# Bank copies of ScalarE placed ahead of roundings, and residuals one product earlier, in a decoder block's second FFN projection

## The chip, the core and the metric

The kernel runs on one core of a Trainium2 chip. The metric is the device time of one execution in microseconds; before, it is 822.0 us, the median of three runs (821.88 to 822.13). The core's engines work side by side, each through its own queue of instructions in program order: TensorE (PE, matmuls; PEld is its weight load), VectorE (DVE), ScalarE (ACT), GpSimd (POOL) and SyncE (SP, which here only issues DMAs).

## What is computed

One decoder layer on 512 positions of width 1024: two mixers side by side, then a SwiGLU feed-forward network, then a final RMSNorm. The change touches the last part only, from the end of the first FFN matmul on:

```python
    h2 = rms_norm(x, norm2_g) * (1.0 + scale2) + shift2
    f_g, f_u = jnp.split(h2 @ w_ffn_in, 2, axis=-1)
    x = x + gate2 * ((jax.nn.silu(f_g) * f_u) @ w_ffn_out)
    return x
...
    return rms_norm(x, final_norm_g)
```

`w_ffn_out` has 2816 rows and 1024 columns. All of it is float32.

## The kernel before

**Precision.** A float32 product is made of three matmuls in a rounded format (`mm3`, lines 51 to 55). Each operand is split: `hi` is the value rounded, a copy by ScalarE; `lo` is the value less `hi`, a subtraction by VectorE. The matmuls are hi x hi, hi x lo and lo x hi, all adding into one PSUM bank. So every piece of weights and of activations needs a rounding on ScalarE and a subtraction on VectorE ahead of its matmuls.

**Weights.** `ensure` (119) walks a list of weight chunks of 512 KB. `issue` (72) starts the DMA of a chunk on SP into one of three buffers `raw`; `prep` (95) rounds it (line 112, ScalarE) and subtracts (line 116), into `hi` and `lo` of three buffers each. So a chunk's rounding can begin when the chunk three places before it has been multiplied, and a load when the subtraction of the chunk three places before it is done. `get(i, ahead)` (144) makes sure that chunk `i` and the `ahead` chunks behind it are prepared.

**First FFN projection.** The loop `for q in range(-2, NQ)` (1642), makes each group of columns by a Strassen-like scheme of seven products in place of eight (`sprod`, 1636). Partial sums are carried from one PSUM bank to the next: ScalarE copies bank `R[0]` into `R[1]` (1676) and `R[1]` into `R[2]` (1689), and TensorE adds the next product to the copy. The preparations for the next group, `pre`, are set between these steps; in the last group (q = 17) `pre` comes from `z_first` (1595), which prepares the second projection: the first three weight chunks (`b(0)` to `b(2)`) and the parts 0 to 2 of the activations `A11`, rounded by `a_hi` (1569; line 1585 in the profile) and subtracted by `a_lo` (1587; 1589). `a_sum` (1593 in the profile) makes a difference of two activation blocks for a later product.

**Second FFN projection.** Again seven products (`zprod`, 1760), in this order: A11, S1, S2, A12, S3, A22, S4. Each goes over six chunks of weights (c = 0 to 5; the last is half as long), and for each chunk over two halves e of 128 rows with 512 columns each. One chunk is 12 matmuls, the last 6. Ahead of the matmuls of chunk c stand `get`, which by default prepares the chunk two further on, and then a list of tasks written out by hand for that c: roundings, subtractions, sums, residuals. The results gather in the banks `Z[k][e]`. `z_copy` (1770) seeds a bank from another one; `z_out` (1775, the copy is line 1779) copies two banks, e = 0 and e = 1, to SBUF, because `z_add` (1781) needs them and TensorE goes on adding to the same banks. After product S3, `z_out(2)` does this, and product A22 adds to the same two banks `Z[2]`.

**Residual, norm and output.** For row block tk (128 rows) and column half h, `res_(tk, h)` (1827) runs `resid_v` (1234): VectorE multiplies the bank by the gate (1238) and adds into `xt[tk]` (1239); the square with its sum, on ScalarE (1240), is put on a list that `sq_` (1834) empties. `scale_g` (1724; 1730 in the profile) multiplies by the final norm's gain. `row_rstd` (1246) reduces the sums of a row block on VectorE (1247) and raises them to -1/2 on GpSimd (1248). `scaled(tk, n)` (1732) scales the row block: the columns from n on by ScalarE (1735), the first n by VectorE (1736); then it issues two output DMAs, one on SP and one on ScalarE's queue (1739). After the third chunk of S4 the last three chunks are prepared together (`ch`, 1844) and multiplied for row block 0 as a whole (512 columns) and for row block 1 in two halves of 256; for the second half a bank is copied first (1842). Each of these three is followed by its residual, and at the very end by `finish` (1741).

In a profile a helper's instructions carry the helper's line. The functions that the diff touches, with their line numbers:

Of the kernel before, what the change touches and what calls it, by code (L numbers as in the profile page):

```python
# [28 lines left out]
def block_kernel(ctx: ExitStack, tc: tile.TileContext, x, positions, w_ada, b_ada, w_in,  # L29
# [28 lines left out]
    stream, wseq, chunk = [], [], {}  # L58
# [60 lines left out]
    def ensure(upto):  # L119
        upto = min(upto, len(stream) - 1, st["limit"] - 1)  # L120
        while True:
            for i in range(st["prep"], min(st["prep"] + 16, len(stream), st["limit"])):
                if "raw" in stream[i]:
                    continue
                if room(i):
                    issue(i)
                elif stream[i]["kind"] == "w" or not stream[i]["mid"]:
                    break
            if st["prep"] > upto:
                break  # L130
# [139 lines left out]
    NZ = 6  # L270
# [3 lines left out]
    W_Z = {}  # L274
# [75 lines left out]
    def t512(name, dt=F32):  # L350
        return base.tile([128, 512], dt, name=name, tag="t512", bufs=3)
# [65 lines left out]
    gate_b = {1: base.tile([128, D], F32, name="gate1b", tag="gate", bufs=1)}  # L417
# [120 lines left out]
    for kt in range(8):  # L538
# [7 lines left out]
        kw = dict(skip_group_check=True)  # L546
# [687 lines left out]
    def resid_v(p, c0, n, slot, tk, gate):  # L1234

        cs_ = slice(c0, c0 + n)
        t = t512("rt")
        V.tensor_mul(t[:, :n], p, gate[:, cs_])
        V.tensor_add(xt[tk][:, cs_], xt[tk][:, cs_], t[:, :n])
        return lambda: A.activation(t[:, :n], xt[tk][:, cs_], AF.Square, scale=1.0 / 32,  # L1240
                                    accum_out=ss2[:, tk, slot:slot + 1])
# [4 lines left out]
    def row_rstd(tk):  # L1246
        V.tensor_reduce(r2[:, tk:tk + 1], ss2[:, tk], op=OP.add, axis=AX.X)
        P.tensor_tensor(r2[:, tk:tk + 1], r2[:, tk:tk + 1], mhalf[:, :1], op=OP.pow)
# [312 lines left out]
    def a_part(name, c):  # L1561
        kh, th = AT_[name]
        t = gz[((0, 1, 3, 5), (2, 4, 3, 5))[kh][c]]
        if c >= 2:
            n = 4 - c
            t = t[:, n * kh:n * kh + n]
        return t[:, :, th * 256:(th + 1) * 256]

    def a_hi(key, c):
        h = (ZA[key] + (None,))[c]  # L1570
        if c == 3:
            if not zl:
# [12 lines left out]
        A.activation(t[0], a_part(key, c), AF.Copy)  # L1585

    def a_lo(key, c):
        hi, lo = za[key, c]
        V.tensor_sub(lo, a_part(key, c), f(hi))

    def a_sum(key, c):
        x_, y_ = {"S1": ("A21", "A22"), "S2": ("A11", "S1"), "S3": ("S2", "A22"), "S4": ("A12", "S2")}[key]
        V.tensor_sub(*(a_part(n, c) for n in (key, x_, y_)))

    def z_first():
        def b(k):
            return lambda: ensure(wseq[wseq.index(W_Z[0, 0][0]) + k])
        st["limit"] = 1 << 30
        return [(b(0), lambda: a_hi("A11", 0), lambda: a_lo("A11", 0)),
                (b(1), lambda: a_hi("A11", 1), lambda: a_lo("A11", 1)),  # L1600
                (lambda: a_hi("A11", 2), lambda: (a_lo("A11", 2), a_sum("S2", 0))),
                (b(2), lambda: None)]


    pf = [[bank(b, "pf") for b in bs] for bs in ((0, 1), (2, 3))]
# [36 lines left out]
    for q in range(-2, NQ):  # L1642
        g, u = 2 + q // 2, q % 2
# [4 lines left out]
        S2_, S1_, A12, A22, S4_, S3_ = (half_of(d[k], e) for k in "CBD" for e in range(2))  # L1648
# [75 lines left out]
    def scale_g(c0, n, tk):  # L1724
        if not xo:
            for k in range(2):
                t = ffn[0].tile([128, 2, D], F32, name="xo", tag=f"E{k + 1}", bufs=1)
                xo.extend((t[:, 0], t[:, 1]))
        cs_ = slice(c0, c0 + n)
        V.tensor_mul(xo[tk][:, cs_], xt[tk][:, cs_], fng[0][:, cs_])  # L1730

    def scaled(tk, n):

        if n < D:
            A.activation(xo[tk][:, n:], xo[tk][:, n:], AF.Copy, scale=r2[:, tk:tk + 1])
        V.scalar_tensor_tensor(xo[tk][:, :n], xt[tk][:, :n], r2[:, tk:tk + 1], fng[0][:, :n],
                               op0=OP.mult, op1=OP.mult)
        for c, q in ((slice(0, 512), SY), (slice(512, D), A)):
            q.dma_start(out[tk * 128:(tk + 1) * 128, c], xo[tk][:, c])
# [8 lines left out]
    Z, ZB = {}, ((4, 7), (0, 1), (2, 3), (5, 6))  # L1748
# [8 lines left out]

    ALL = slice(0, 512)

    def zprod(k, ka, kw, start, tasks):  # L1760
        if start:
            Z[k] = [bank(ZB[k][e], "pfo") for e in range(2)]
        for c, i in enumerate(W_Z[kw][:len(tasks)]):
            w = get(i)
            for fn in tasks[c]:
                fn()
            for e in range(2):
                zmm(Z[k][e], ka, c, e, w, ALL, start and c == 0, c == NZ - 1)
# [3 lines left out]
        for e in range(2):  # L1772
            A.activation(Z[dst][e], Z[src][e], AF.Copy, scale=scale)

    def z_out(src):
        Z["s", src] = [t512("ps") if src == 3 else base.tile([128, 512], F32, name="ps", tag="acc", bufs=2)
                       for _ in range(2)]
        for e in range(2):
            A.activation(Z["s", src][e], Z[src][e], AF.Copy)  # L1779

    def z_add(dst, src, op):
        for e in range(2):
            op(Z[dst][e], Z[dst][e], Z["s", src][e])

    def hi_(key, c):
        return lambda: a_hi(key, c)

    def lo_(key, c):
        return lambda: a_lo(key, c)
# [10 lines left out]
    def load_fng():  # L1800
        fng.append(ffn[0].tile([128, D], F32, name="fng", tag="E0", bufs=1))
        P.dma_start(fng[0], rows_bcast(final_norm_g, D))

    zprod(0, "A11", (0, 0), True, [[outs_left, hi_("S1", 0)], [lo_("S1", 0), hi_("S1", 1), hi_("A11", 3)],
                                   [lo_("S1", 1), lo_("A11", 3), hi_("S1", 2), sm_("S2", 1)],
                                   [lo_("S1", 2), sm_("S1", 3), sm_("S2", 2), hi_("S2", 0)],
# [9 lines left out]
    zprod(0, "A12", (1, 0), False, [[lo_("A12", 3), hi_("S3", 2)], [lo_("S3", 2), lambda: z_add(1, 3, V.tensor_add)],  # L1816
                                    [hi_("A22", 0)], [lo_("A22", 0), hi_("A22", 1)], [lo_("A22", 1), hi_("A22", 2)],
                                    [lo_("A22", 2)]])
    zprod(2, "S3", 3, False, [[hi_("S3", 3), load_fng], [lo_("S3", 3), hi_("S4", 0)], [lo_("S4", 0), hi_("S4", 1)],
                              [lo_("S4", 1), hi_("S4", 2)], [lo_("S4", 2), hi_("A22", 3)], [lo_("A22", 3)]])  # L1820
    z_out(2)
    z_add(3, 2, V.tensor_sub)


    sq = []

    def res_(tk, h, g=True):
        def fn():
            sq.append(resid_v((Z[h] if tk < 2 else Z[2 + h])[tk % 2], 512 * h, 512, h, tk, gate_b[2]))
            if g:  # L1830
                scale_g(512 * h, 512, tk)
        return fn

    def sq_():
        while sq:
            sq.pop(0)()

    zprod(2, "A22", 4, False, [[res_(0, 0)], [sq_, res_(1, 0)], [sq_], [res_(2, 1)], [sq_, hi_("S4", 3)], [lo_("S4", 3)]])

    zprod(1, "S4", (1, 1), False, [[res_(3, 1, False)], [sq_, res_(2, 0, False)], [sq_, res_(3, 0, False)]])  # L1840
    last = bank(7, "pfo")
    A.activation(last[:, :256], Z[1][1][:, 256:], AF.Copy)
    ids = W_Z[1, 1][3:]
    ch = [get(i, 2 - k) for k, i in enumerate(ids)]
    sq_()
    row_rstd(2)
    row_rstd(3)
    scaled(2, 512)
    scaled(3, D)
    for tk in range(2):  # L1850
        for z in range(2) if tk else (None,):
            c = ALL if z is None else slice(256 * z, 256 * z + 256)
# [74 lines left out]
```

## Time and profile before

| | |
|---|---|
| median of three runs | 822.0 us (821.88 to 822.13) |
| the profiled execution | 823.29 us |
| its span, first to last instruction | 821.5 us |
| granted TensorE clock, mean | 0.998 |
| TensorE busy in the span | 805.9 us, 98% |
| VectorE / ScalarE / GpSimd busy | 686.6 / 430.9 / 166.6 us |

The trace is one execution. A row of a timeline reads: start in us from the span's start, duration in us, engine, line, operation, output tile and input tile with their shapes, count, and in brackets the idle time ahead of it and what ended that. Consecutive rows of one engine overlap by some hundredths or, on TensorE, by more, since instructions are pipelined; so times are also read from start to start. A row of the waits reads: engine, line, what it waited for, then the sum in us, how often, and the longest.

### The profile page before, as it was taken

The page shows a single profiled execution, that of the slowest core. Times are in us where ns is not written, and L with a number is a line of the kernel's source. Part 1 is how long each engine was busy: PE and PEld are TensorE (multiplying, and loading weights), DVE is VectorE, ACT ScalarE, POOL GpSimd, SP SyncE. Part 2 cuts the span into 40 slices and gives each one's busy share as a digit, 9 for nine tenths or more (in the row PEclk, how much of TensorE's full clock was granted, in tenths as well). Part 3 has the DMA queues.
Part 4 walks back from the last instruction along what each step waited for, and adds up shares of the span by engine and source line. Part 5 has one row for each costly group of instructions (what it writes and reads, how often), then busy time and mean ns, then how long its engine had stood idle before and what let it go on. Part 6 is the DMA issues. An engine that isn't in the chain of part 4 may idle for free.

```text
span 821.5 us, 12945 instructions
## 1 busy us (share of the span) xinstructions
PE 805.9 (98%) x4903; PEld 719.6 (88%) x4903; DVE 686.6 (84%) x1175; ACT 430.9 (52%) x772; POOL 166.6 (20%) x186
## 2 busy tenths in 40 slices
PE   7999999999999999999999999999999999999996
PEld 6789889988888888988888899999999999888875
DVE  7989798898899648888697879889999888898686
ACT  6674445322332226665635587555555655666554
POOL 3060031363344411000010010323121322000001
PEclk9999999999999999999999999999999999999999
DMA  9974352332346563037692603989997977556763
GB/s 294 301 222 111 111 180 78 104 102 79 106 150 198 166 200 102 28 104 247 195 254 48 205 27 103 227 236 250 255 280 196 247 182 207 172 190 201 219 175 134
DMA packets 108463, 141.35 MB, mean 172 GB/s; under 512 B 6689, under 2 KB 77089, under 8 KB 108209
## 3 DMA queue, kind: packets, MB, share of 16 engines
q1 hardware_dynamic: 97296, 110.41, 43.4%
q0 software_dynamic: 10384, 29.17, 15.0%
q10 hardware_dynamic: 720, 0.95, 0.3%
q8 instruction: 38, 0.62, 0.3%
q14 instruction: 25, 0.20, 0.1%
HBM read 138.15 MB, written 25.17 MB: 199 GB/s over the span
## 4 chain that ended last, share of the span: by engine, by line
PE 79%; DMA 7%; DVE 7%; ACT 4%; issue 1%; SPq 1%; POOL 0%; POOLq 0%; ACTq 0%; DVEq 0%
PE R L53 8%; PE R L54 8%; PE R L55 8%; PE pb L53 6%; PE pb L54 6%; PE pb L55 6%; PE pfo L53 4%; PE pfo L55 4%; PE pfo L54 4%; DMA mraw<-in_w_ada_dram 3%; PE pav L54 2%; PE pav L53 2%; PE pav L55 2%; DMA s<-in_w_ada_dram 2%; DMA oraw<-in_w_out_dram 2%; PE pgb L53 2%
## 5 line engine op out<-in xcount | busy, mean ns | idle before, releaser
L112 ACT ACTIVATE hi<-raw 128x1024 fp32r<-128x1024 f32 (+2 forms) x108 | 109.3, 1013 | 105.6 <-PE pfo L55 22.0
L116 DVE TENSOR_TENSOR lo<-raw,hi 128x1024 fp32r<-128x1024 f32 (+2 forms) x72 | 83.5, 1163 | 24.3 <-ACT hi L112 23.9
L116 POOL TENSOR_TENSOR lo<-raw,hi 128x1024 fp32r<-128x1024 f32 x29 | 73.4, 2533 | 128.1 <-ACT hi L112 122.4
L53 PE MATMUL pb<-h,hi 128*128 128x512 f32 (+1 forms) x192 | 74.5, 388 | 0.0
L55 PE MATMUL pb<-h,lo 128*128 128x512 f32 (+1 forms) x192 | 73.9, 385 | 0.0
L54 PE MATMUL pb<-h,hi 128*128 128x512 f32 (+1 forms) x192 | 73.9, 385 | 0.0
L53 PE MATMUL pfo<-hi,za 128*128 128x512 f32 (+1 forms) x144 | 55.9, 388 | 0.3 <-ACT ps L1779 0.3
L55 PE MATMUL pfo<-hi,za 128*128 128x512 f32 (+1 forms) x144 | 55.8, 388 | 0.0
L54 PE MATMUL pfo<-lo,za 128*128 128x512 f32 (+1 forms) x144 | 55.8, 388 | 0.0
L177 DVE SCALAR_TENSOR_TENSOR acc<-mraw,cols,acc 128x512 f32<-128x512 f32 x49 | 39.5, 807 | 18.5 <-DMA mraw<-in_w_ada_dram 17.5
L53 PE MATMUL R<-tb,sx 128*128 128x256 f32 x160 | 45.3, 283 | 0.3 <-ACT R L1689 0.3
L54 PE MATMUL R<-tb,sx 128*128 128x256 f32 x160 | 45.1, 282 | 0.0
L322 POOL COPY sm<-sm 128x1 f32<-128x1 f32 x36 | 26.0, 723 | 93.7 <-ACT sm L321 93.7
L55 PE MATMUL R<-tb,sx 128*128 128x256 f32 x160 | 45.0, 281 | 0.0
L55 PE MATMUL R<-tb,lo 128*128 128x256 f32 x160 | 44.8, 280 | 0.0
L53 PE MATMUL R<-tb,hi 128*128 128x256 f32 x160 | 44.8, 280 | 0.0
L54 PE MATMUL R<-tb,hi 128*128 128x256 f32 x160 | 44.6, 279 | 0.0
L55 PEld LDWEIGHTS pb<-h,lo 128*128 128x128 f32 x192 | 36.0, 188 | 7.3
L54 PEld LDWEIGHTS pb<-h,hi 128*128 128x128 f32 x192 | 36.0, 188 | 6.9
L53 PEld LDWEIGHTS pb<-h,hi 128*128 128x128 f32 x192 | 36.0, 188 | 6.8
L302 POOL DMA_DIRECT2D wsum<-in_w_ffn_out_dram x24 | 21.2, 888 | 73.1 <-DMA wsum<-wsum 45.2
L54 PE MATMUL pav<-lo,h 128*128 128x256 f32 x128 | 35.8, 279 | 0.0
(387 smaller groups left out, 2656.2 us busy)
## 6 DMA issues: line engine op xcount, KB each, us to landing
raw<-in_w_ffn_in_dram SPq DMA_DIRECT2D x44, 512.0 KB, 5.9
raw<-in_w_in_dram SPq DMA_DIRECT2D x40, 512.0 KB, 3.9
wsum<-in_w_ffn_out_dram POOLq DMA_DIRECT2D x30, 512.0 KB, 8.2
mraw<-in_w_ada_dram SPq DMA_DIRECT2D x28, 512.0 KB, 4.0
raw<-wsum SPq DMA_DIRECT2D x20, 512.0 KB, 3.7
raw<-in_w_ffn_out_dram SPq DMA_DIRECT2D x16, 512.0 KB, 4.5
s<-in_w_ada_dram SPq DMA_DIRECT2D x30, 256.0 KB, 5.5
wsum<-wsum POOLq DMA_DIRECT2D x10, 512.0 KB, 5.6
```

The source lines that it names most:

```text
L53: T.matmul(o, wh, rh, start=start, stop=False, **kw)
L54: T.matmul(o, wh, rlo, start=False, stop=False, **kw)
L55: T.matmul(o, wlo, rh, start=False, stop=stop, **kw)
L112: A.activation(hi[:, :m], e["raw"][:, :m], AF.Copy)
L116: e["lo"].tensor_sub(lo[:, :m], e["raw"][:, :m], f(hi[:, :m]))
L177: V.scalar_tensor_tensor(o, w, cs[:, j:j + 1], o, op0=OP.mult, op1=OP.add)
L302: P.dma_start(wsum[n][o], src, accum_op=OP.add)
L322: P.tensor_copy(t, t)
```

## The change

It has four parts.

- `z_first`: rounding and subtraction of A11's part 1 move from the slot behind the second product of the last group to the slot behind the copy of `R[1]` into `R[2]`, and part 2 with the sum moves on to the last slot.
- `zprod` gets a parameter `ahead` for the last chunk of a product, and `z_out` a callback `between`. Product S3 is called with `ahead=1`, so that its last chunk prepares one chunk less; that chunk is prepared between the two copies of `z_out(2)`.
- The residuals of row blocks 0 and 1 for column half 0 move from product A22 into product S3 (without their `scale_g`, which stays in A22); the residual (3, 1) moves from S4 into A22, and (2, 0) and (3, 0) move one chunk forward within S4.
- `row_rstd(2)` and `row_rstd(3)` move into the tasks of S4's third chunk, and `scaled(2, 512)` ahead of the bank copy 1842 and of the preparation of the last chunks.

```diff
@@ z_first
         return [(b(0), lambda: a_hi("A11", 0), lambda: a_lo("A11", 0)),
-                (b(1), lambda: a_hi("A11", 1), lambda: a_lo("A11", 1)),
-                (lambda: a_hi("A11", 2), lambda: (a_lo("A11", 2), a_sum("S2", 0))),
-                (b(2), lambda: None)]
+                (b(1),),
+                (lambda: a_hi("A11", 1), lambda: a_lo("A11", 1)),
+                (lambda: (b(2)(), a_hi("A11", 2)), lambda: (a_lo("A11", 2), a_sum("S2", 0)))]
@@ zprod
-    def zprod(k, ka, kw, start, tasks):
+    def zprod(k, ka, kw, start, tasks, ahead=2):
...
-            w = get(i)
+            w = get(i, ahead if c == NZ - 1 else 2)
@@ z_out
-    def z_out(src):
+    def z_out(src, between=lambda: None):
...
             A.activation(Z["s", src][e], Z[src][e], AF.Copy)
+            if e == 0:
+                between()
@@ the products
-    zprod(2, "S3", 3, False, [[hi_("S3", 3), load_fng], [lo_("S3", 3), hi_("S4", 0)], [lo_("S4", 0), hi_("S4", 1)],
-                              [lo_("S4", 1), hi_("S4", 2)], [lo_("S4", 2), hi_("A22", 3)], [lo_("A22", 3)]])
-    z_out(2)
+    zprod(2, "S3", 3, False, [[hi_("S3", 3), load_fng], [lo_("S3", 3), hi_("S4", 0), res_(0, 0, False)],
+                              [lo_("S4", 0), hi_("S4", 1)], [sq_, lo_("S4", 1), hi_("S4", 2), res_(1, 0, False)],
+                              [lo_("S4", 2), hi_("A22", 3)], [lo_("A22", 3)]], 1)
+    z_out(2, lambda: ensure(wseq[wseq.index(W_Z[4][0]) + 1]))
     z_add(3, 2, V.tensor_sub)
...
-    zprod(2, "A22", 4, False, [[res_(0, 0)], [sq_, res_(1, 0)], [sq_], [res_(2, 1)], [sq_, hi_("S4", 3)], [lo_("S4", 3)]])
+    zprod(2, "A22", 4, False, [[sq_, lambda: scale_g(0, 512, 0)], [lambda: scale_g(0, 512, 1)], [res_(2, 1)], [sq_],
+                               [res_(3, 1, False), hi_("S4", 3)], [sq_, lo_("S4", 3)]])
 
-    zprod(1, "S4", (1, 1), False, [[res_(3, 1, False)], [sq_, res_(2, 0, False)], [sq_, res_(3, 0, False)]])
+    zprod(1, "S4", (1, 1), False, [[res_(2, 0, False)], [sq_, res_(3, 0, False)],
+                                    [sq_, lambda: row_rstd(2), lambda: row_rstd(3)]])
+    scaled(2, 512)
     last = bank(7, "pfo")
     A.activation(last[:, :256], Z[1][1][:, 256:], AF.Copy)
     ids = W_Z[1, 1][3:]
     ch = [get(i, 2 - k) for k, i in enumerate(ids)]
-    sq_()
-    row_rstd(2)
-    row_rstd(3)
-    scaled(2, 512)
     scaled(3, D)
```

More of the change, by code (lines that the diff above doesn't have):

```diff
@@ L1802, in load_fng, with res_, fn, sq_ @@
         P.dma_start(fng[0], rows_bcast(final_norm_g, D))
+    sq = []
+    def res_(tk, h, g=True):
+        def fn():
+            sq.append(resid_v((Z[h] if tk < 2 else Z[2 + h])[tk % 2], 512 * h, 512, h, tk, gate_b[2]))
+            if g:
+                scale_g(512 * h, 512, tk)
+        return fn
+    def sq_():
+        while sq:
+            sq.pop(0)()
     zprod(0, "A11", (0, 0), True, [[outs_left, hi_("S1", 0)], [lo_("S1", 0), hi_("S1", 1), hi_("A11", 3)],
@@ L1818, in block_kernel @@
                                     [lo_("A22", 2)]])
-    zprod(2, "S3", 3, False, [[hi_("S3", 3), load_fng], [lo_("S3", 3), hi_("S4", 0)], [lo_("S4", 0), hi_("S4", 1)],
-                              [lo_("S4", 1), hi_("S4", 2)], [lo_("S4", 2), hi_("A22", 3)], [lo_("A22", 3)]])
-    z_out(2)
+    zprod(2, "S3", 3, False, [[hi_("S3", 3), load_fng], [lo_("S3", 3), hi_("S4", 0), res_(0, 0, False)],
+                              [lo_("S4", 0), hi_("S4", 1)], [sq_, lo_("S4", 1), hi_("S4", 2), res_(1, 0, False)],
+                              [lo_("S4", 2), hi_("A22", 3)], [lo_("A22", 3)]], 1)
+    z_out(2, lambda: ensure(wseq[wseq.index(W_Z[4][0]) + 1]))
     z_add(3, 2, V.tensor_sub)
[L1825 to L1836, printed above, removed]
-    zprod(2, "A22", 4, False, [[res_(0, 0)], [sq_, res_(1, 0)], [sq_], [res_(2, 1)], [sq_, hi_("S4", 3)], [lo_("S4", 3)]])
-    zprod(1, "S4", (1, 1), False, [[res_(3, 1, False)], [sq_, res_(2, 0, False)], [sq_, res_(3, 0, False)]])
+    zprod(2, "A22", 4, False, [[sq_, lambda: scale_g(0, 512, 0)], [lambda: scale_g(0, 512, 1)], [res_(2, 1)], [sq_],
[3 more added lines that the diff above has]
+    scaled(2, 512)
     last = bank(7, "pfo")
```

## The prediction

> **What bounds the kernel now.** I read the chain that ended last first, then the waits of TensorE in the stretch that the change touches (695 us to the end), then the timelines of each engine around those waits and in the tail.
>
> ```profile
> PE 79%; DMA 7%; DVE 7%; ACT 4%; issue 1%; SPq 1%; POOL 0%; POOLq 0%; ACTq 0%; DVEq 0%
> PE R L53 <- ACT R L1689: 0.3, 1, 0.3
> PE pfo L53 <- ACT ps L1779: 0.3, 1, 0.3
> ```
>
> The first line is the chain by engine: TensorE carries 79% of it, so removed work of another engine pays only where TensorE stood still for it. The other two are all the waits of TensorE that the trace names after 695 us: two, once each, both for a ScalarE copy of a PSUM bank. Everywhere else in this stretch matmuls start every 0.23 us (512 columns) or 0.12 us (256), and the rest runs under them until the tail, where VectorE sets the end. So the change has three places to act: wait one, wait two, the tail.
>
> Wait one, on TensorE and on ScalarE:
>
> ```profile
> 700.83 0.28 PE L55 MATMUL R<-h,sx 128*128 128x256 f32 x1
> 701.43 0.39 PE L53 MATMUL R<-tb,sx 128*128 128x256 f32 x1 [0.33 <-ACT R L1689]
> 701.66 0.28 PE L54 MATMUL R<-tb,sx 128*128 128x256 f32 x1
> ```
>
> ```profile
> 699.01 1.06 ACT L112 ACTIVATE hi<-raw 128x1024 fp32r<-128x1024 f32 x1
> 699.96 1.06 ACT L1585 ACTIVATE za<-gq 128x1024 fp32r<-128x1024 f32 x1
> 700.91 0.20 ACT L321 ACTIVATE sm<-cols 128x1 f32<-128x1 f32 x1
> 701.00 0.38 ACT L1689 ACTIVATE R<-R 128x256 f32<-128x256 f32 x1
> ```
>
> TensorE would have gone on at 700.83 + 0.12 = 700.95; it started at 701.43, and the next matmul came 0.23 later instead of 0.12. The bare gap is 0.48 us, and with the slow first matmul 0.48 + 0.11 = 0.59. The bank copy L1689 was late because the rounding of A11's part 1 (L1585) stood ahead of it: 0.95 us from start to start.
>
> Wait two:
>
> ```profile
> 781.33 0.39 PE L55 MATMUL pfo<-hi,zl 128*128 128x512 f32 x1
> ...
> 782.01 0.39 PE L55 MATMUL pfo<-hi,zl 128*128 128x512 f32 x1
> 782.66 0.50 PE L53 MATMUL pfo<-hi,za 128*128 128x512 f32 x1 [0.27 <-ACT ps L1779]
> 783.00 0.40 PE L54 MATMUL pfo<-lo,za 128*128 128x512 f32 x1
> ```
>
> ```profile
> 781.07 1.06 ACT L112 ACTIVATE hi<-raw 128x1024 fp32r<-128x1024 f32 x1 [1.44 <-PE pfo L55]
> 782.03 1.07 ACT L1779 ACTIVATE ps<-pfo 128x512 f32<-128x512 f32 x2
> L1779 ACT ACTIVATE ps<-pfo x4: 578/584/592, 736.1 to 782.5; 128x512 f32<-128x512 f32 x4
> ```
>
> The half e=0 of product S3 is complete when the matmul of 781.33 ends, 781.72. Its copy started only at 782.03, behind a weight rounding (L112). TensorE could have gone on at 782.01 + 0.23 = 782.24, started at 782.66, and lost another 0.34 - 0.23 = 0.11 on the first matmul: 0.42 + 0.11 = 0.53.
>
> **Part one, z_first: -0.59.** One rounding (L1585) and its VectorE subtraction go behind the bank copy; nothing is added. ScalarE then runs rounding 699.01, the small L321 at 699.96 (0.09 start to start), the copy at 700.05, done 700.43. TensorE wants it at 700.95, so 0.52 is to spare and the stall goes. The copy's input is ready: it comes from the product before the twelve matmuls that end with the row at 700.83. What is later instead: part 1 is rounded from 700.34 and part 2 and the sums after it move back on VectorE by about 1.2 us (one subtraction of 1.22 changes places with the chunk's). The cover is VectorE's gap ahead of the next chunk:
>
> ```profile
> 709.90 1.23 DVE L116 TENSOR_TENSOR lo<-raw,hi 128x1024 fp32r<-128x1024 f32 x1 [1.85 <-ACT hi L112]
> 773.76 1.23 DVE L116 TENSOR_TENSOR lo<-raw,hi 128x1024 fp32r<-128x1024 f32 x1 [1.24 <-ACT hi L112]
> ```
>
> 1.85 us idle, of which 0.59 goes as TensorE arrives earlier and 1.2 to the shift: nothing is left over, but what comes next there is a chunk that TensorE reads two chunks later (two times twelve matmuls of 0.23, 5.6 us). Without that cover a late chunk would cost up to 1.2. Bounds: 0.48 (bare gap) to 0.59; I take 0.59, since the slow first matmul stands in both stalls.
>
> **Part two, z_out: -0.29.** With `ahead=1` no weight rounding is queued in S3's last step; the copy of e=0 starts at 781.72 + 0.03 = 781.75, and 0.58 later TensorE gets its bank: 782.33, and starts 0.04 after (as 782.62 to 782.66 before), at 782.37. Gain 782.66 - 782.37 = 0.29; 0.13 of gap and the slow first matmul stay. The rounding now stands between the copies. Its start-to-start time is 0.96 (781.07 to 782.03), a copy's 0.48, so the copy of e=1 starts at 781.75 + 0.48 + 0.96 = 783.19 and ends at 783.77. TensorE needs e=1 after six matmuls, 782.37 + 0.34 + 5 x 0.23 = 783.86. A margin of 0.09 less 0.04 for the handover: 0.05. If it is missed, another slow first matmul comes, 0.11 and a little gap, some 0.2 together. The weight chunk rounded there loses 1.2 us of lead of two products; no DMA is pushed past another, as all of them go through SP in the same order. Bounds: 0.08 (margin missed) to 0.42 (the whole gap, with the slow first matmul left). I take 0.29.
>
> **The residuals in the middle: 0.** Two residuals (0,0 and 1,0) move into product S3: a multiply and an add each on VectorE, 1.45 together (a residual of this size runs from 805.98 to 807.43 in the tail's rows below), and a square on ScalarE. VectorE idles 1.24 ahead of 773.76 and as much at the other chunks of S3; the first residual overruns by 0.2, on a chunk that TensorE reads two steps later. Without cover each would be 1.45. In products A22 and S4 VectorE gets room in return, but TensorE waits for nothing there now, so that room is worth nothing until the tail.
>
> **The tail: -0.05.** Last residual of row block 3, statistics of blocks 2 and 3, their scaling and output:
>
> ```profile
> 806.50 0.37 ACT L1842 ACTIVATE pfo<-pfo 128x256 f32<-128x256 f32 x1 [1.00 <-PE pfo L55]
> 806.78 0.62 ACT L112 ACTIVATE hi<-raw 128x512 fp32r<-128x512 f32 x1
> ...
> 808.87 0.72 ACT L1735 ACTIVATE xo<-xo,sm 128x512 f32<-128x512 f32 x1 [0.72 <-POOL sm L1248]
> 809.62 0.36 ACTq L1739 DMA_DIRECT2D out_dram<-xo  x1
> ```
>
> ```profile
> 804.84 1.23 DVE L116 TENSOR_TENSOR lo<-raw,hi 128x1024 fp32r<-128x1024 f32 x1
> 805.98 0.68 DVE L1238 TENSOR_TENSOR rt<-pfo,gate2b 128x512 f32<-128x512 f32 x1
> ...
> 807.43 0.69 DVE L116 TENSOR_TENSOR lo<-raw,hi 128x512 fp32r<-128x512 f32 x1
> 808.04 0.36 DVE L1247 TENSOR_REDUCE sm<-ss 128x1 f32<-128x5 f32 x2
> 808.87 1.95 DVE L1736 SCALAR_TENSOR_TENSOR xo<-xr,sm,fng 128x512 f32<-128x512 f32 x2 [0.47 <-POOL sm L1248]
> 810.74 0.68 DVE L1238 TENSOR_TENSOR rt<-pfo,gate2b 128x512 f32<-128x512 f32 x1
> L1736 DVE SCALAR_TENSOR_TENSOR xo<-xr,sm,fng x2: 752/1016/1279, 808.9 to 809.5; 128x512 f32<-128x512 f32 x1, 128x1024 f32<-128x1024 f32 x1
> 808.28 1.08 POOL L1248 TENSOR_TENSOR sm<-sm,mhalf 128x1 f32<-128x1 f32 x2 [49.78 <-DVE sm L1247]
> 809.29 0.39 PE L54 MATMUL pfo<-lo,zl 128*128 128x512 f32 x1
> 809.51 0.40 PE L55 MATMUL pfo<-hi,zl 128*128 128x512 f32 x1
> ```
>
> Now: block 0's sum is complete at 809.51 + 0.40 = 809.91, but its residual starts at 810.74, because VectorE first ran the last chunk's low part, the reductions, and the two scalings (1.95). So at most 810.74 - 809.91 = 0.83 can be won.
>
> After, with TensorE's times kept as they are (the 0.88 of parts one and two moves all of this alike): the reduction for block 2 follows the low part of 804.84, at 805.98, where the residual was. From the reduction to the released scaling was 808.87 - 808.04 = 0.83, so the scaling's half on ScalarE (0.72) starts at 806.81 and ends at 807.53. But it and its output DMA are now queued ahead of the bank copy L1842 and the last chunk's rounding. DMA issue at 807.56, 0.37 to 807.93; copy 807.96; rounding 0.28 later at 808.24, done 808.86; the low part on VectorE 808.88 to 809.57. TensorE wanted it at 809.29 (the matmul that reads lo): a new stall of 0.31, with the slow start 0.42, block 0 complete at 810.33. On VectorE the 1024-wide scaling starts 0.61 after the low part (807.43 to 808.04), at 809.49, and the residual follows 1.28 - 0.08 later (0.08 is the overlap 808.87 + 1.95 against 810.74): 810.69. Against 810.74 this wins 0.05. The later chain to the last store is VectorE's and unchanged.
>
> The cost that decides is ScalarE's DMA issue, which stands ahead of the rounding only in the new order. The trace has one issue with work right behind it:
>
> ```profile
> 0.73 0.41 ACTq L151 DMA_DIRECT2D cols<-in_small_dram  x1
> 1.17 1.28 ACT L337 ACT_TABLE_LOAD   x1 [1.17 <-PEq L1904]
> ```
>
> ScalarE's next work starts 0.03 after the 0.41 window ends, so I take the whole window as held. The Trainium skill's Perfetto Trace Analysis, section "DMA Instruction — HWDGE (DVE, Sync)", says the sequencer is free for the next instruction only at the end of that window; the trace agrees. The Trainium skill's DMA: Bandwidth & Descriptors, "Anatomy of one DMA — SWDGE (gpsimd) path", gives about 50 ns for a sequencer's dispatch, for GpSimd's path; by it the tail would win 0.32 more and the time would be an estimated 820.8. Bounds of the tail without it: +0.49 (ScalarE's half waits for both of GpSimd's powers: 0.54, half of the 1.08 of the two in the GpSimd row) to -0.42 (the issue holds nothing: 0.05 + 0.37).
>
> **Sum.** 0.59 + 0.29 + 0.05 = 0.93 us. The profiled execution took 823.29 with a span of 821.5, 1.79 around it; after: 820.57 and 822.36. Its time is 1.29 above the median 822.0, so the median goes to 822.0 - 0.93 = **821.1**. From the bounds, gains of 0.48 + 0.08 - 0.49 = 0.07 to 0.59 + 0.42 + 0.42 = 1.43: 820.6 to 821.9.
>
> **Rivals.**
> *The tail is freed as well.* If the last chunk's rounding does not end up behind the scaling on ScalarE, block 0's residual starts when TensorE is done: 0.59 + 0.42 + 0.83 = 1.84, 820.2. For it: VectorE then has a free stretch from 806.8 on. Against it: program order on ScalarE, which the trace shows kept everywhere.
> *The stalls only move.* TensorE, no longer waiting for these copies, waits as long for the next late item (part 2 of A11, or the copy of e=1), and the tail gains nothing: 822.0. For it: margins of 0.05 at e=1 and of nothing on VectorE at 709. Against it: no rounding of A11 is needed before TensorE has run some 5 us of part 0.
> *Slower: the last chunk is held on ScalarE.* Every microsecond that the output's issue or the wait for GpSimd's power holds ScalarE beyond my 0.37 delays the rounding, the low part, the 1024-wide scaling and block 0's residual one for one. From 0.93 on it is slower than before; if the issue holds the queue until the data has landed (2.8 us by the table of DMA issues), it costs 2.43 more: 821.1 + 2.4 = 823.5. Against it: the row at 1.17 us, which started while the load that was issued at 0.73 was still under way. *The copies are not ahead after all* falls under the second rival: same time as before.
>
> ```profile
> out_dram<-xo ACTq DMA_DIRECT2D x2, 256.0 KB, 2.8
> ```
>
> **How the numbers follow.** Forecast 0.60; stalls only move 0.12; tail freed 0.12; slower 0.16. A measurement of this kernel tells about 0.2%, 1.64 us, from no change: faster means under 820.36, slower over 823.64. The forecast and the moved stalls lie within; of the slower case I put 0.10 beyond 823.64, since more than one hold can add up there, and 0.06 within. So faster 0.12, same 0.60 + 0.12 + 0.06 = 0.78, slower 0.10. The range runs from 820.2, the freed tail, to 822.4, past the moved stalls and the first part of the slower case; the forecast's own is 820.6 to 821.9.
>
> **What would show it.** Right: no wait of TensorE for L1689's copy; the wait at z_out's copy near 0.1 and none at e=1; a new short wait of TensorE for the last chunk's low part near the end; ScalarE running scaling, issue, copy, rounding in this order; block 0's residual about 4.2 us after the end of S4's third step, as now (806.50 to 810.74). Wrong: a wait at pfo early in the first product, a ScalarE gap longer than 0.4 behind the output's issue, or a residual that starts as TensorE ends.

## The result, and the profile after

| | before | after |
|---|---|---|
| median, us (22 executions each) | 822.17 (821.56 to 825.03) | 820.85 (820.20 to 821.75) |
| the profiled execution, us | 823.29 | 820.46 |
| its span, us | 821.5 | 818.7 |

The ratio is 0.9982 (95% interval 0.9975 to 0.9988): 1.48 us less (0.99 to 2.06) of before's 822.17. That is under the 0.2% that I took as no change, though the interval lies wholly below 1. The two medians themselves differ by 1.32. The forecast was 0.93 less, to 821.1.

The two traces differ by 2.83 us, but most of that lies where nothing was changed. TensorE's first matmul of the last group of the first projection (q = 17), from the timelines of before and then of after:

```profile
695.24 0.28 PE L53 MATMUL R<-h,sa 128*128 128x256 f32 x1
```

```profile
692.88 0.28 PE L53 MATMUL R<-h,sa 128*128 128x256 f32 x1
```

Up to here the instructions are the same and after is already 2.36 ahead. In all the traces of this text the same matmul starts between 692.62 (change_early) and 696.01 (residuals_only), though no edit reaches ahead of it. So spans of two traces cannot be compared here, and I measure from this matmul to VectorE's last scaling (line 1743): 816.57 - 695.24 = 121.33 before, 813.74 - 692.88 = 120.86 after, 0.47 less in this pair. VectorE's timelines of before and of after have these ends:

```profile
816.57 0.55 DVE L1743 TENSOR_SCALAR xo<-xo,sm 128x640 f32<-128x640 f32 x1 [0.45 <-POOL sm L1875]
```

```profile
813.74 0.55 DVE L1743 TENSOR_SCALAR xo<-xo,sm 128x640 f32<-128x640 f32 x1 [0.45 <-POOL sm L1877]
```

**The waits.** The waits of TensorE in after, from 695 us on, are one row:

```profile
PE pfo L54 <- DVE lo L116: 0.2, 1, 0.2
```

The two waits for ScalarE's bank copies are gone from the list, and the new one is the one for the last chunk's low part that the prediction named, 0.23 where it had 0.31. Counted from start to start TensorE lost more there, 0.85 where the working had 0.42: the starts in the tail's rows below lie 0.47 (from 805.65 to 806.12, where the rounded half of the chunk came late as well), 0.73 and 0.34 apart in place of 0.23 each.

**Wait one.** ScalarE in after, at the copy of `R[1]` into `R[2]`:

```profile
697.60 0.20 ACT L321 ACTIVATE sm<-cols 128x1 f32<-128x1 f32 x1
697.69 0.38 ACT L1689 ACTIVATE R<-R 128x256 f32<-128x256 f32 x1
697.99 1.05 ACT L1585 ACTIVATE za<-gq 128x1024 fp32r<-128x1024 f32 x1
```

The copy (1689) now stands ahead of the rounding (1585). TensorE goes from the last group's first matmul to the first one of A11 in 9.98 in place of 10.57: the whole 0.59. A11's first matmul, in before and then in after:

```profile
705.81 0.40 PE L53 MATMUL pfo<-hi,za 128*128 128x512 f32 x1
```

```profile
702.86 0.40 PE L53 MATMUL pfo<-hi,za 128*128 128x512 f32 x1
```

**Wait two.** ScalarE and then TensorE in after, at the end of S3:

```profile
778.80 0.60 ACT L1779 ACTIVATE ps<-pfo 128x512 f32<-128x512 f32 x1 [2.07 <-PE pfo L55]
779.30 1.05 ACT L112 ACTIVATE hi<-raw 128x1024 fp32r<-128x1024 f32 x1
780.24 0.59 ACT L1779 ACTIVATE ps<-pfo 128x512 f32<-128x512 f32 x1
```

```profile
779.06 0.39 PE L55 MATMUL pfo<-hi,zl 128*128 128x512 f32 x1
779.45 0.50 PE L53 MATMUL pfo<-hi,za 128*128 128x512 f32 x1
779.79 0.40 PE L54 MATMUL pfo<-lo,za 128*128 128x512 f32 x1
...
780.72 0.40 PE L55 MATMUL pfo<-hi,za 128*128 128x512 f32 x1
780.96 0.43 PE L53 MATMUL pfo<-hi,za 128*128 128x512 f32 x1
781.22 0.39 PE L54 MATMUL pfo<-lo,za 128*128 128x512 f32 x1
```

From S3's last matmul to A22's first it is 0.39, where it was 0.65: 0.26 won. The second copy starts 1.44 after the first, as worked out (0.48 + 0.96). At e = 1 the matmuls stand 0.24 and 0.26 apart instead of 0.23, so 0.03 or 0.04 is lost, in place of the 0.2 that I had put on a missed margin. By its row the second copy ends at 780.83, 0.13 ahead of the matmul at 780.96 and so not too late by the working; what takes the 0.03 is not shown.

**The tail.** ScalarE, TensorE and VectorE in after:

```profile
800.91 1.06 ACT L112 ACTIVATE hi<-raw 128x1024 fp32r<-128x1024 f32 x1 [0.60 <-DMA raw<-in_w_ffn_out_dram]
...
803.97 0.72 ACT L1735 ACTIVATE xo<-xo,sm 128x512 f32<-128x512 f32 x1 [1.20 <-POOL sm L1248]
804.73 0.35 ACTq L1739 DMA_DIRECT2D out_dram<-xo  x1
805.13 0.37 ACT L1848 ACTIVATE pfo<-pfo 128x256 f32<-128x256 f32 x1 [0.43 <-ACT xo L1735]
805.44 0.63 ACT L112 ACTIVATE hi<-raw 128x512 fp32r<-128x512 f32 x1
```

```profile
802.88 0.40 PE L55 MATMUL pfo<-hi,za 128*128 128x512 f32 x1
...
806.12 0.50 PE L53 MATMUL pfo<-hi,zl 128*128 128x512 f32 x1
806.85 0.51 PE L54 MATMUL pfo<-lo,zl 128*128 128x512 f32 x1 [0.23 <-DVE lo L116]
```

```profile
802.00 1.23 DVE L116 TENSOR_TENSOR lo<-raw,hi 128x1024 fp32r<-128x1024 f32 x1
...
806.10 0.69 DVE L116 TENSOR_TENSOR lo<-raw,hi 128x512 fp32r<-128x512 f32 x1 [1.37 <-ACT hi L112]
806.71 1.28 DVE L1736 SCALAR_TENSOR_TENSOR xo<-xr,sm,fng 128x1024 f32<-128x1024 f32 x1
807.91 0.68 DVE L1238 TENSOR_TENSOR rt<-pfo,gate2b 128x512 f32<-128x512 f32 x1
```

The order on ScalarE is the one predicted: scaling, issue, copy, rounding, low part, scaling of block 3, residual of block 0. The matmul of 802.88 is the last of S4's third chunk; from it to block 0's residual (807.91) it is 5.03, where before had 4.68 (806.06 to 810.74). The matmul in before's timeline:

```profile
806.06 0.40 PE L55 MATMUL pfo<-hi,za 128*128 128x512 f32 x1
```

So this trace gained 0.59 + 0.23 ahead of the tail and gave 0.35 back in it. That the rounding of 800.91 waited for a DMA is what the experiments had to explain, and with it why the median gained 1.48 where this pair shows 0.47.

### The profile page after: what moved, and what is told of

It is laid out like the page before. It is cut to its first block, busy times and chain, and to the rows that moved or that the text cites. A ratio compares the mean times of both kernels' runs of the same rounds, so it can differ in the third digit from the quotient of the medians.

```text
span 818.7 us, 12943 instructions
## 1 busy us (share of the span) xinstructions
PE 804.8 (98%) x4903; PEld 719.3 (88%) x4903; DVE 686.5 (84%) x1175; ACT 431.3 (53%) x772; POOL 162.0 (20%) x186
## 4 chain that ended last, share of the span: by engine, by line
PE 93%; DMA 3%; DVE 2%; ACT 1%; issue 0%; SPq 0%; POOL 0%; POOLq 0%; ACTq 0%; DVEq 0%
PE pb L53 9%; PE pb L55 9%; PE pb L54 9%; PE R L53 8%; PE R L54 8%; PE R L55 8%; PE pfo L53 3%; PE pfo L55 3%; PE pfo L54 3%; PE pav L54 2%; PE pav L53 2%; PE pav L55 2%; PE pgb L53 2%; PE pgb L54 2%; PE pgb L55 2%; PE po L54 2%
## 5 line engine op out<-in xcount | busy, mean ns | idle before, releaser
L322 POOL COPY sm<-sm 128x1 f32<-128x1 f32 x36 | 23.5, 653 | 90.1 <-ACT sm L321 90.0
```

The lines of the kernel that those rows point to most:

```text
L322: P.tensor_copy(t, t)
```

## The experiments

The runs came in three lots, each beside its own runs of before. Columns of the table, from timelines, in us: **P**, from the last group's first matmul to A11's first; **gap**, from S3's last matmul to A22's first; **load**, issue on SP of S4's first weight chunk, counted from A22's first matmul; **rounding**, start of ScalarE's rounding of that chunk, counted likewise; **tail**, from the last matmul of S4's third chunk to block 0's residual; **total**, as above, to line 1743; and the ratio of the times to before, with its interval.

| kernel | P | gap | load | rounding | tail | total | ratio |
|---|---|---|---|---|---|---|---|
| before | 10.57 | 0.65 | 6.61 | 11.56 | 4.68 | 121.33 | |
| after | 9.98 | 0.39 | 6.25 | 12.16 | 5.03 | 120.86 | 0.9982 (0.9975 to 0.9988) |
| zfirst_only | 9.98 | 0.65 | 6.61 | 12.78 | 6.04 | 122.08 | 0.9994 (0.9985 to 1.0002) |
| zout_only | 10.58 | 0.39 | 7.70 | 13.86 | 6.04 | 123.31 | 1.0013 (1.0004 to 1.0022) |
| residuals_only | 10.57 | 0.65 | 5.46 | 11.40 | 4.69 | 121.35 | 0.9999 (0.9990 to 1.0007) |
| both_copies | 9.98 | 0.40 | 7.69 | 13.08 | 6.19 | 122.08 | 1.0000 (0.9991 to 1.0009) |
| before_again | 10.57 | 0.66 | 6.60 | 11.71 | 4.67 | 121.33 | 0.9993 (0.9985 to 1.0002) |
| early_load | 10.56 | 0.66 | 3.80 | 11.40 | 4.68 | 121.32 | 0.9990 (0.9979 to 1.0000) |
| scaling_behind | 9.98 | 0.40 | 6.24 | 12.13 | 3.89 | 119.77 | 0.9975 (0.9966 to 0.9983) |
| behind_and_early | 9.98 | 0.40 | 4.89 | 11.44 | 3.89 | 119.76 | 0.9976 (0.9967 to 0.9984) |
| change_early | 9.99 | 0.40 | 4.89 | 11.44 | 4.70 | 121.49 | 0.9983 (0.9974 to 0.9992) |
| copies_early | 9.98 | 0.40 | 4.90 | 11.44 | 4.67 | 120.70 | 0.9992 (0.9983 to 1.0001) |
| before_late | 10.56 | 0.65 | 6.61 | 11.99 | 4.68 | 121.32 | 0.9995 (0.9986 to 1.0003) |
| change_late | 9.98 | 0.40 | 6.25 | 11.63 | 4.84 | 120.70 | 0.9988 (0.9980 to 0.9997) |

The columns from P to total are one traced execution per kernel; the ratio is from all executions.

### The parts alone

zfirst_only has the first hunk of the change alone. zout_only has the second part alone:

```diff
-    z_out(2)
+    z_out(2, lambda: ensure(wseq[wseq.index(W_Z[4][0]) + 1]))
```

with `zprod`'s `ahead`, S3's `1` and `between` as in the change. residuals_only has the task lists, `scale_g`, `row_rstd` and `scaled(2, 512)` where the change puts them, with the copies as before. both_copies is the first two together.

> Only the edit of z_first is made. Theory 'what the traces show': the stretch from the first matmul of the last group (q = 17) to the first matmul of product A11 goes from 10.57 to 9.98 us, wait two stays at 0.65 from the last matmul of S3 to the first of A22, the tail from the last matmul of S4's third chunk to block 0's residual stays at 4.68; the time falls by 0.6 us, ratio 0.9993. Rival 'the stall only moves': a wait of TensorE of about 0.6 us appears in product A11, ratio 1.0000.

> Only ahead=1 in product S3 and the chunk between the copies of z_out(2). Theory 'what the traces show': last matmul of S3 to the first of A22 goes from 0.65 to 0.39 us and the half e=1 is at most 0.03 late, so the time falls by 0.23 us, ratio 0.9997; the first stretch stays at 10.57 and the tail at 4.68. Rival 'margin missed': e=1 waits 0.1 to 0.2 us and nothing is won, ratio 1.0000.

> Only the moves of residuals, row_rstd and scaled(2, 512). Theory 'what the traces show': no gain up to the tail, and the tail from the last matmul of S4's third chunk to block 0's residual grows from 4.68 to about 5.0 us, because the last chunk is rounded behind the scaling on ScalarE and the chunk before it arrives later; ratio 1.0004. Rival 'the residuals carry the measured gain': the tail shortens in the median execution and this kernel alone is faster by 0.5 to 0.9 us, ratio 0.9990 to 0.9994.

> The edits of z_first and z_out together, residuals and tail as before the change. Theory 'what the traces show': 0.59 + 0.23 = 0.82 us less than before the change, ratio 0.9990, and faster than the whole change by the 0.35 us that its tail lost. Rival 'the residuals carry the measured gain': slower than the whole change (0.9982) by 0.5 us or more, ratio 0.9990 with the whole change at 0.9984.

P and the gap came out as expected in every kernel, whatever else it had: 0.59 and 0.25 or 0.26. The totals did not, and neither did the tail of residuals_only (4.69 where about 5.0 was expected). zfirst_only wins 0.59 and loses 1.36 in the tail; zout_only is slower than before. SP and ScalarE around S4's first weight chunk, first in before, then zfirst_only, then zout_only:

```profile
789.27 0.37 SPq L92 DMA_DIRECT2D raw<-in_w_ffn_out_dram  x1
794.22 1.06 ACT L112 ACTIVATE hi<-raw 128x1024 fp32r<-128x1024 f32 x1 [2.25 <-DMA raw<-in_w_ffn_out_dram]
```

```profile
787.50 0.37 SPq L92 DMA_DIRECT2D raw<-in_w_ffn_out_dram  x1
793.67 1.06 ACT L112 ACTIVATE hi<-raw 128x1024 fp32r<-128x1024 f32 x1 [3.47 <-DMA raw<-in_w_ffn_out_dram]
...
803.47 1.06 ACT L112 ACTIVATE hi<-raw 128x1024 fp32r<-128x1024 f32 x1 [1.86 <-DMA raw<-in_w_ffn_out_dram]
```

```profile
788.59 0.37 SPq L92 DMA_DIRECT2D raw<-in_w_ffn_out_dram  x1
794.75 1.06 ACT L112 ACTIVATE hi<-raw 128x1024 fp32r<-128x1024 f32 x1 [3.58 <-DMA raw<-in_w_ffn_out_dram]
```

Two things are to be seen. The load took 4.95 from issue to rounding in before (794.22 - 789.27), 6.17 in zfirst_only, whose instructions are the same there. both_copies and zout_only, of one lot, issue it at the same point (7.69 and 7.70) and show 5.39 and 6.16. So its length scatters by about a microsecond without an edit that explains it. And in zout_only it was issued 7.70 after A22's first matmul, in before 6.61 (789.27 - 782.66). That second difference is not scatter: both_copies has 7.69, and zfirst_only and before_late, without the z_out part, 6.61. The chunk between the two copies is subtracted in A22 where its subtraction began in S3, VectorE in A22 is full of residuals, and so every subtraction there comes 1.1 later. A load is issued when a subtraction frees its buffer: in zout_only the one that starts at 787.35 ends at 788.57, and the issue stands at 788.59.

From there on lateness is handed on: rounding late, subtraction late, the load three places on late. In zfirst_only it arrives at the chunk that is rounded at 803.47, the last whole one, 0.82 before the third chunk's last matmul (804.29); in before that distance is 2.31 (803.75 to 806.06). The load of that chunk in before and then in zfirst_only:

```profile
799.13 0.37 SPq L92 DMA_DIRECT2D raw<-in_w_ffn_out_dram  x1
```

```profile
797.89 0.37 SPq L92 DMA_DIRECT2D raw<-in_w_ffn_out_dram  x1
```

Counted from A22's first matmul it is issued only 0.53 later (17.00 against 16.47), but it lands 5.5 after its issue, in before 4.2. The load ahead of it was issued 1.87 before it, in before 2.56. That the two loads slowed each other would fit, but no run separates this from scatter. So the larger part of the lateness is that load's own length, not what was handed on to its issue. TensorE and VectorE then have this in zfirst_only:

```profile
804.29 0.40 PE L55 MATMUL pfo<-hi,za 128*128 128x512 f32 x1
```

```profile
804.56 1.23 DVE L116 TENSOR_TENSOR lo<-raw,hi 128x1024 fp32r<-128x1024 f32 x1 [0.98 <-ACT hi L112]
805.70 0.68 DVE L1238 TENSOR_TENSOR rt<-pfo,gate2b 128x512 f32<-128x512 f32 x1
806.42 0.69 DVE L1239 TENSOR_TENSOR xr<-xr,rt 128x512 f32<-128x512 f32 x1
...
808.46 1.95 DVE L1736 SCALAR_TENSOR_TENSOR xo<-xr,sm,fng 128x512 f32<-128x512 f32 x2 [0.33 <-POOL sm L1248]
810.33 0.68 DVE L1238 TENSOR_TENSOR rt<-pfo,gate2b 128x512 f32<-128x512 f32 x1
```

Same instructions as before's tail, but the subtraction starts 0.27 after the third chunk's last matmul (804.56 - 804.29), in before 1.22 ahead of it (804.84 to 806.06). Nothing between there and block 0's residual could take up the 1.49, and 1.36 of it arrived. In zout_only TensorE itself had to wait as well, 0.56, for S4's first low part; the waits of TensorE in that trace:

```profile
PE pfo L54 <- DVE lo L116: 0.6, 1, 0.6
```

With the residuals moved (residuals_only) the load is issued at 5.46, and the tail is 4.69: 0.01 longer than before. So alone they win nothing, and the tail order wins nothing. But set on top of both copies they bring the issue from 7.69 back to 6.25, and the tail from 6.19 to 5.03. The medians agree: the parts alone give 0.9994, 1.0013 and 0.9999, the copies together 1.0000, all of it 0.9982.

### Is it the load?

Theory: what the tail loses hangs on when S4's first chunk arrives. Rival: it hangs on the order of the tail's instructions. early_load (on before), change_early (on after) and copies_early (on both_copies) give that chunk a buffer of its own, so that its DMA and those of the next chunks are issued one subtraction earlier:

```diff
+        elif W_Z and i == W_Z[1, 1][0]:
+            raw = ffn[0].tile([128, 1024], F32, name="raw", tag="F0", bufs=1)
...
+        if W_Z and st["prep"] <= W_Z[1, 1][0] <= i:
+            return len(pend) < RAWB + 1
```

before_late and change_late put a load of another 512 KB, which nothing reads, behind it:

```diff
+        if W_Z and i == W_Z[1, 1][0]:
+            other = ffn[0].tile([128, 1024], F32, name="other", tag="F0", bufs=1)
+            SY.dma_start(other.rearrange("p (j n) -> p j n", j=2),
+                         w_ffn_out[0:256, 0:512].rearrange("(j p) n -> p j n", p=128))
```

before_again is before once more, to show what a repeated kernel gives.

> The kernel before once more, unchanged, as a second trace of it. Theory 'late load': the tail of an execution depends on how long the first weight load of product S4 takes (4.9 us in the first trace of before, 6.1 and 6.2 in the two kernels with only one of the copies moved), so from the first matmul of the last group to the final scaling it takes between 121.3 (load 5 us) and 122.7 us (load over 6 us), without any change of code. Rival 'the edits did it': 121.3 again whatever the load took. Ratio 1.0000 with an interval of about 0.0009 to both sides.

> The kernel before, with one edit: the first weight load of S4 goes into a fourth buffer (free after product S3), so it is issued some 3 us earlier and the loads behind it one buffer earlier. Theory 'late load': ScalarE no longer waits for a load in S4, the tail is that of the good execution of before or better (first 256-column matmul to block 0's residual 0.5 to 1.0 us, not 2.0), and the time falls by 0.5 to 1.0 us, ratio 0.9988 to 0.9994. Rival 'VectorE is full anyway': loads earlier, but the residuals on VectorE still set the tail; ratio 1.0000.

> The whole change with the fourth buffer for S4's first load and nothing else. Theory 'late load': without the late load the tail is the one that the prediction worked out, 0.05 under that of before, so from the first matmul of the last group to the final scaling it takes 121.33 - 0.59 - 0.23 - 0.05 = 120.46 us (the traced change had 120.86, with a load of 5.9), with a wait of TensorE for the last chunk's low part of about 0.3; ratio 0.9978 to 0.9983. Rival 'the queue on ScalarE alone made the 0.35': 120.86 again.

> Both copies moved, no residual moved, and the fourth buffer for S4's first load. Theory 'late load': the tail is that of before, 0.99 us from the first 256-column matmul to block 0's residual and not the 1.99 of the kernel with both copies alone; the stretch takes 121.33 - 0.82 = 120.5 us, against 122.08 there; ratio 0.9985 to 0.9991. Rival 'moving the copies itself makes VectorE late in S4': 122 again, ratio 1.0000.

> The kernel before, and directly behind S4's first load a second load of 512 KB that nothing reads, so that the first one shares the DMA engines and lands later. Theory 'late load': landing after 6 us or more, and the stretch from the first matmul of the last group to the final scaling grows from 121.33 to 122.5 or 123 us, ratio 1.0010 to 1.0020. Rival 'VectorE's order alone sets the tail': 121.33 still.

> The whole change with the same second load. Theory 'late load': with three residuals gone from product S4 and the end of A22, VectorE makes up for a late load, so the stretch grows by less than in the kernel before, from 120.86 to at most 121.4 us, and the ratio to the kernel before with the same load would be about 0.998 or less; to the kernel before 0.9982 to 0.9990. Rival 'the residuals bring no slack': the same growth as there, 1.2 us or more.

copies_early settles this in the traces. It is both_copies with the earlier loads alone; ScalarE rounds the chunk at 11.44 in place of 13.08, and no longer waits for a DMA there (its timeline, where the rounding is line 115):

```profile
791.86 1.06 ACT L115 ACTIVATE hi<-raw 128x1024 fp32r<-128x1024 f32 x1 [1.16 <-issue]
```

Its tail is 4.67 against 6.19, its total 120.70 against 122.08. (By the times, 0.9992 and 1.0000, the intervals overlap.) In change_early the tail is 4.70 against after's 5.03. So the rival falls for these differences: the order was the same within each pair. It does not say that the first chunk alone counts: the last whole chunk's load is issued 16.51 after A22's first matmul in place of 17.31 as well, and lands 3.5 after its issue in place of 5.4.

Read down the table, the tail is long where the first chunk's rounding is late. With the residuals where they were it is 4.67 or 4.68 up to 11.99, and 6.04 or more from 12.78 on. With them moved it is 4.69 and 4.70 up to 11.44, 4.84 at 11.63 and 5.03 at 12.16 (scaling_behind apart, below): that order feels a late rounding sooner, and what it has ahead of both_copies is the earlier issue. Close to the end it is nearly one for one: the subtraction of the last whole chunk starts 1.22 ahead of the third chunk's last matmul in before, 0.88 ahead in after (802.00 to 802.88) and 0.27 behind it in zfirst_only, and the tails are 4.68, 5.03 and 6.04.

The misses. early_load won nothing that the times can tell (its interval ends at 1.0000, and before_again, the same kernel as before, lies at 0.9993), since the traces of before have the load in time anyway. The extra load of before_late and change_late did not make the chunk late: 5.38 from issue to rounding in both, within the 4.95 to 6.17 seen without it, so the pair did not test what it was for. And change_early's total is 121.49 although its tail is good, because of another late load, that of the third weight chunk of A11. ScalarE there, and then the waits of TensorE:

```profile
703.37 1.06 ACT L115 ACTIVATE hi<-raw 128x1024 fp32r<-128x1024 f32 x1 [3.04 <-DMA raw<-in_w_ffn_out_dram]
```

```profile
PE pfo L54 <- DVE lo L119: 0.9, 2, 0.7
```

One of the two waits is the tail's 0.23; the other, 0.66 at 719.02, is at the second matmul of product S1. The third chunk is rounded 10.75 after the last group's first matmul, in after 8.43 (701.31 in its timeline). VectorE has no idle time from that chunk's subtraction on, so S1's first low part comes 2.33 later than in after (its subtraction starts at 25.13 in place of 22.80), and there TensorE runs into it. This is what the prediction's "nothing is left over" on VectorE leads to. Gaps between matmul starts price it at 0.92; without it the total would be 120.57. In copies_early the same matmul comes late too, which costs 0.15. The other six traces with part one show nothing there.

### Is the tail held on ScalarE?

The prediction's working said that 0.83 lies in the tail, and that ScalarE's scaling and DMA issue ahead of the last rounding keep the change from winning it. scaling_behind is the whole change with VectorE's half of the scaling left where the change puts it, and ScalarE's half and both DMAs behind the bank copy and the last rounding:

```diff
-    scaled(2, 512)
+    V.scalar_tensor_tensor(xo[2][:, :512], xt[2][:, :512], r2[:, 2:3], fng[0][:, :512], op0=OP.mult, op1=OP.mult)
     last = bank(7, "pfo")
...
     ch = [get(i, 2 - k) for k, i in enumerate(ids)]
+    A.activation(xo[2][:, 512:], xo[2][:, 512:], AF.Copy, scale=r2[:, 2:3])
+    for c, q in ((slice(0, 512), SY), (slice(512, D), A)):
+        q.dma_start(out[256:384, c], xo[2][:, c])
     scaled(3, D)
```

behind_and_early adds the earlier load to it.

> The whole change, but the ScalarE half of scaled(2, 512) and its two output DMAs stand behind the bank copy and the last chunk's rounding; the VectorE half stays ahead. Theory 'the last chunk queued behind the scaling costs the tail': the wait of TensorE for the last chunk's low part (0.23 us) goes, block 0's residual starts within 0.1 us of the first 256-column matmul plus 0.2, the time falls by 0.5 to 0.8 us against the whole change: ratio 0.9973 to 0.9977 to before. Rival 'VectorE sets the tail': no difference from the whole change, 0.9982.

> The whole change with both of the above: the scaling behind the last chunk, and the fourth buffer for S4's first load. Theory 'late load' and theory 'queued behind' together: no wait of ScalarE for a load in S4 and none of TensorE in the tail, 0.3 to 0.5 us under the kernel with the scaling behind alone, ratio 0.9967 to 0.9973. Rival: with the residuals moved the loads have slack already, and the fourth buffer adds nothing.

ScalarE and then VectorE in scaling_behind:

```profile
804.12 0.37 ACT L1848 ACTIVATE pfo<-pfo 128x256 f32<-128x256 f32 x1 [0.59 <-PE pfo L55]
804.40 0.62 ACT L112 ACTIVATE hi<-raw 128x512 fp32r<-128x512 f32 x1
804.92 0.71 ACT L1851 ACTIVATE xo<-xo,sm 128x512 f32<-128x512 f32 x1
805.66 0.35 ACTq L1853 DMA_DIRECT2D out_dram<-xo  x1
```

```profile
805.42 0.68 DVE L116 TENSOR_TENSOR lo<-raw,hi 128x512 fp32r<-128x512 f32 x1
806.03 1.28 DVE L1736 SCALAR_TENSOR_TENSOR xo<-xr,sm,fng 128x1024 f32<-128x1024 f32 x1
807.57 0.69 DVE L1238 TENSOR_TENSOR rt<-pfo,gate2b 128x512 f32<-128x512 f32 x1 [0.26 <-PE pfo L55]
```

Now block 0's residual waits for TensorE, not for VectorE. The tail is 3.89, 0.79 less than before's 4.68 and 1.14 less than after's 5.03, and that with the chunk's rounding as late as in after (12.13). The list of TensorE's waits from 695 us on is empty. The ratio to before is 0.9975 (0.9966 to 0.9983), 2.06 us: this version's time lies below both kernels', though its interval overlaps that of the change (0.9975 to 0.9988, from another lot), so only the trace shows the difference between them surely. The earlier load adds nothing to it (0.9976): with the order mended, VectorE has room for the lateness.

## Why the prediction was right

**Part one, 0.59.** Right to the hundredth, by the steps given. The cover on VectorE was indeed used up: on a late load this cost TensorE 0.92 in one trace and 0.15 in another, of eight that have part one. The prediction had named a late chunk as a cost, but looked for it near 709; it came at the start of S1.

**Part two, 0.29.** 0.26 at the gap and some 0.03 given back at e = 1, so 0.23. The copies' starts were right; TensorE started 0.03 later than worked out.

**The residuals in the middle, 0.** This is the step that was wrong in its reason, if not in its sum, together with a sentence of part two. "The weight chunk rounded there loses 1.2 us of lead of two products; no DMA is pushed past another" was true of the order of the DMAs, but not of their time: the lost lead went down VectorE's queue in A22 and put S4's first load 1.09 later. And the room that the residuals leave in A22 and S4 is not "worth nothing until the tail": without it the copies' gain is lost again (both_copies, 1.0000), with it it stays. Part two and the residual moves belong together, and I had costed them as if each stood alone. Nor does VectorE idle "as much at the other chunks of S3": before's timeline has 1.20, 1.24 and 1.40 ahead of three of them and nothing ahead of two. The two residuals still fitted, and TensorE waits for nothing in S3.

**The tail, -0.05.** With the load in time it is 4.69 and 4.70 against 4.68: next to nothing, as the working said, and some 0.06 off it. In after's own trace, where S4's first load took 5.91 from issue to rounding, that became a loss of 0.35. The chain on ScalarE and VectorE is as worked out there too: from the reduction (803.14) to block 0's residual it takes 4.77, where the working has 4.71 (805.98 to 810.69). What is lost is the 0.34 by which the subtraction ahead of it starts later. The queue of ScalarE is held for the whole window of the issue, as taken: the row at 804.73 lasts 0.35, to 805.08, and the copy starts at 805.13. The Trainium skill's Perfetto Trace Analysis, section "DMA Instruction — HWDGE (DVE, Sync)", says the same of the sequencer, and this trace agrees with it in a place where it decides.

**The sum.** Gains of 0.59 + 0.23 - 0.01 make 0.81 with the load in time, where 0.93 was forecast; 0.47 in the one trace. The measured 1.48 (0.99 to 2.06) is larger than both. What stays open is that difference, 0.67 with the load in time. One reading is chance: before_again, which is before unchanged, came out at 0.9993, so the same kernel taken twice can differ by 0.6. Another is the load: before's load can be as long as zfirst_only's, since the instructions up to there are the same but for the order at A11, and then before would lose the 1.36 that zfirst_only lost; a share of such executions would lengthen before's median. after issues the load 0.36 earlier, and in its trace 5.91 from issue to rounding cost 0.35. But both traces of before that I have show the load in time, and residuals_only, which would be safe from it, shows no gain (0.9990 to 1.0007). The spread of the times (highest 825.03 before, 821.75 after) does not decide it either: two of the longest profiled executions, 823.29 of before and 824.08 of residuals_only, have short tails (4.68 and 4.69) and are long ahead of the last group, whose first matmul starts at 695.24 and 696.01. So neither reading is shown.

**The rivals.** The freed tail did not come with the change, for the reason given against it; scaling_behind shows that the 0.83 was there (0.79 won) and that ScalarE's order alone kept it. Moved stalls were seen twice, 0.92 in change_early and 0.15 in copies_early. The slower case did not come: the issue held ScalarE for 0.35, not until the data had landed.

## What to carry to other kernels

Before a preparation is moved past a product, follow the buffer that it frees: here 1.1 us more on a full VectorE became 1.1 us on the issue of a load two products on, and with the scatter of the loads on top 1.4 to 1.5 on the tail (zout_only and both_copies). Parts of a change that take lead and parts that give it must be costed together. And on an engine that both rounds and issues output DMAs, put the scaling and its issue behind the last rounding that TensorE needs: that was worth 0.8 us here, as much as the two stalls together.

## What the hardware showed beside this

The same 512 KB load, issued by the same instruction, took from 4.95 to 6.17 us from its issue to the rounding that waited for it (before and zfirst_only), with the same instructions on all engines for some 70 us ahead of it. And a matmul stream that pauses pays once more when it starts: in every trace the first matmul of A22, which stands behind a gap of 0.39 to 0.66, keeps the next one 0.33 or 0.34 away (779.45 to 779.79 in after) in place of 0.23.
